# One row of the first group is loaded over the scalar queue, and the sync queue's loads have 32 and 32 rows

## The chip, the cores and the metric

The kernel runs on one core of one Trainium2 chip. A core has several engines that run their own instruction streams: VectorE (DVE in the profile), ScalarE (ACT), GpSimd (POOL), TensorE (PE, unused here) and SyncE (SP), which here only issues transfers. Transfers between the chip's main memory (HBM, "dram" in the names) and the on-chip memory of 128 partitions run on 16 DMA engines that all queues share. A transfer that SyncE issues goes on queue q1, one that ScalarE issues on queue q10.

The metric is device time in microseconds of one execution. The kernel before took 241.25 us, the median of three runs (240.55, 241.25, 241.26).

## What is computed

For each of 16 x 1024 = 16,384 tokens there are 8 router logits and a row of 512 numbers. The two largest logits give two weights that add up to one, and the row is written out twice, once times each weight, the smaller weight first:

```python
probs = np.exp(router_logits - logits_max)
probs = probs / np.sum(probs, axis=-1, keepdims=True)
topk_indices = np.argsort(probs, axis=-1)[..., -k:]          # k = 2
topk_probs = np.take_along_axis(probs, topk_indices, axis=-1)
topk_probs = topk_probs / np.sum(topk_probs, axis=-1, keepdims=True)
x_expanded = x[:, :, np.newaxis, :].repeat(k, axis=2)
return (x_expanded * topk_probs[..., np.newaxis]).astype(np.float32)
```

Everything is float32: 32 MiB of rows and 0.5 MiB of logits are read and 64 MiB are written.

## The kernel before

The 16,384 tokens are two groups (`GROUPS`, line 42): 65 x 128 tokens, then 63 x 128. In a group each of the 128 partitions has 65 (or 63) consecutive tokens, so "a row" below means one token on every partition: 512 numbers, 2 KB on each partition, 256 KB in all. The rows of a group lie in the tile `xs` (65 rows of space). A second tile, `osp`, has room for 18 rows of output, each twice as long as an input row.

`LOADS` (line 44) cuts a group's rows into transfers: 33 and 32 rows for the first group, 4, 28 and 31 for the second. Line 139 issues them. In the first group both go over the sync queue. Behind the first of them (line 142) the two parts of the logits are issued (lines 144 and 145), also on the sync queue, and `top2_weights` computes the weights `WA` from them: eleven small VectorE instructions, and then two sigmoids on ScalarE (lines 37 and 38). So the order on the sync queue is 33 rows, logits, logits, 32 rows.

`STORES` (line 47) cuts the output of a group into four stores: row from which it starts, number of rows, the tile that holds its output, and the place in that tile. Stores one and three of a group are built in `osp`; stores two and four are built in `xs` itself, over rows that are no longer needed. Line 164 multiplies rows by weights on VectorE, one instruction for each store, except that the third product of a group is cut in two (`FREE`, line 54): its first 2 rows go to a part of `osp` that the first store doesn't use, and the rest waits until the first store has landed. Of the first store's rows ScalarE does the last 5 (2 in the second group) as scaled copies (`ACT_ROWS`, line 156). Line 175 issues each store on the sync queue.

The second group's loads go to places in `xs` whose old contents must have been stored. Its first 4 rows go over the scalar queue (`late`, line 123): ScalarE does a copy that waits for the first group's third store to land (line 128) and then issues the load. The other two are on the sync queue, behind the first group's fourth store; the 28 rows wait for store two, the 31 rows for store four.

The instructions of each engine, and the transfers of each queue, stay in the order in which the program issues them. The fourth product of the first group (rows 49 to 64, `xs` from row 33 on) is the only one that reads row 64, the last of the group.

Of the kernel before, what the change touches and what calls it, by code (L numbers as in the profile page):

```python
# [1 line left out]

# [4 lines left out]

F32 = mybir.dt.float32
ALU = mybir.AluOpType
ACTF = mybir.ActivationFunctionType  # L10
P = 128


def top2_weights(nc, WA, dlt, room, logits, E):

    tt = nc.vector.tensor_tensor
    hi, lo, n = None, None, E  # L20
    while n > 1:
        n //= 2
        if hi is None:
            a, b = logits[:, :, 0:n], logits[:, :, n : 2 * n]
            nhi, nlo = room(n), b
            tt(nhi, a, b, op=ALU.max)  # L26
            tt(nlo, a, b, op=ALU.min)  # L27
        else:
            a, b = hi[:, :, 0:n], hi[:, :, n : 2 * n]
            nhi, nlo, tmp = room(n), room(n), room(n)  # L30
            tt(tmp, lo[:, :, 0:n], lo[:, :, n : 2 * n], op=ALU.max)  # L31
            tt(nlo, a, b, op=ALU.min)  # L32
            tt(nlo, nlo, tmp, op=ALU.max)  # L33
            tt(nhi, a, b, op=ALU.max)  # L34
        hi, lo = nhi, nlo
    tt(dlt, hi[:, :, 0], lo[:, :, 0], op=ALU.subtract)  # L36
    nc.scalar.activation(WA[:, :, 0], dlt, ACTF.Sigmoid, scale=-1.0)  # L37
    nc.scalar.activation(WA[:, :, 1], dlt, ACTF.Sigmoid, scale=1.0)  # L38

GROUPS = [65, 63]

LOADS = [[33, 32], [4, 28, 31]]
BASE = [0, 1]

STORES = [
    [(0, 16, "osp", 2), (16, 16, "xs", 0), (32, 17, "osp", 0), (49, 16, "xs", 33)],
    [(0, 16, "osp", 2), (16, 16, "xs", 0), (32, 15, "osp", 0), (47, 16, "xs", 32)],
]  # L50

L = 18

FREE = [2, 2]

ACT_ROWS = [5, 2]


@with_exitstack
def kernel(  # L60
    ctx: ExitStack,
    tc: tile.TileContext,
    x: bass.AP,
    router_logits: bass.AP,
    k: bass.AP,
    out: bass.AP,
):
    nc = tc.nc
    B, S, D = x.shape
    E = router_logits.shape[-1]  # L70
    N = B * S
    assert int(k) == 2 and E == 8 and N == P * sum(GROUPS)
    M = N // P

    x_v, o_v, rl_v = [], [], []
    t0 = 0
    for n in GROUPS:
        t1 = t0 + P * n
        x_v.append(
            x.rearrange("b s d -> (b s) d")[t0:t1].rearrange("(p m) d -> p m d", p=P)  # L80
        )
        o_v.append(
            out.rearrange("b s k d -> (b s) k d")[t0:t1].rearrange(
                "(p m) k d -> p m k d", p=P
            )
        )
        rl_v.append(
            router_logits.rearrange("b s e -> (b s) e")[t0:t1].rearrange(
                "(p m) e -> p m e", p=P
            )  # L90
        )
        t0 = t1

    wpool = ctx.enter_context(tc.tile_pool(name="wpool", bufs=1))
    xs = wpool.tile([P, max(GROUPS), D], F32)
    osp = wpool.tile([P, L, 2, D], F32)
    WA = wpool.tile([P, M, 2], F32)
    dlt = wpool.tile([P, M], F32)


    flat = osp.rearrange("p l k d -> p (l k d)")
    taken = [0]

    def room(n):
        o = taken[0]
        taken[0] += M * n
        return flat[:, o : o + M * n].rearrange("p (m n) -> p m n", n=n)

    logits = room(E)

    def place(where, at, n):

        if where == "osp":
            return osp[:, at : at + n]
        return xs[:, at : at + 2 * n, :].rearrange("p (r k) d -> p r k d", k=2)

    m0 = 0
    stores = []
    for g, G in enumerate(GROUPS):
        x0, r = BASE[g], 0  # L120
        for n in LOADS[g]:

            late = g == 1 and r == 0
            if late:


                rows = xs[:, x0 : x0 + 2, :]
                pause = nc.scalar.activation(rows, rows, ACTF.Copy)  # L128
                tc.add_manual_dep(
                    pause.ins,  # L130
                    stores[-2].ins.name,
                    mybir.DependencyInfo(
                        mybir.DependencyClass.Sync, mybir.DependencyReason.DATA
                    ),
                    reason="begin when the store ahead of the last has landed",
                )
                tc.keep_in_program_order(pause)
            queue = nc.scalar if late else nc.sync
            load = queue.dma_start(xs[:, x0 + r : x0 + r + n, :], x_v[g][:, r : r + n, :])  # L139
            tc.keep_in_program_order(load)  # L140
            r += n
            if g == 0 and r == LOADS[0][0]:
                n0 = GROUPS[0]
                tc.keep_in_program_order(nc.sync.dma_start(logits[:, :n0], rl_v[0]))  # L144
                tc.keep_in_program_order(nc.sync.dma_start(logits[:, n0:], rl_v[1]))
                top2_weights(nc, WA, dlt, room, logits, E)
        assert r == G
        for r, n, where, at in STORES[g]:
            og = place(where, at, n)

            again = where == "osp" and at == 0 and r > 0
            cuts = [0, FREE[g], n] if again else [0, n]
            if r == 0:
                cuts = [0, n - ACT_ROWS[g]]
                for j in range(n - ACT_ROWS[g], n):
                    for k2 in range(2):
                        nc.scalar.activation(  # L157
                            og[:, j, k2, :],
                            xs[:, x0 + r + j, :],
                            ACTF.Copy,  # L160
                            scale=WA[:, m0 + r + j, k2 : k2 + 1],
                        )
            for a, b in zip(cuts, cuts[1:]):
                nc.vector.tensor_tensor(  # L164
                    og[:, a:b],
                    xs[:, x0 + r + a : x0 + r + b, :]
                    .unsqueeze(2)
                    .to_broadcast([P, b - a, 2, D]),
                    WA[:, m0 + r + a : m0 + r + b, :]
                    .unsqueeze(3)  # L170
                    .to_broadcast([P, b - a, 2, D]),
                    op=ALU.mult,
                )

            stores.append(nc.sync.dma_start(o_v[g][:, r : r + n], og))  # L175
            tc.keep_in_program_order(stores[-1])
        m0 += G


# [1 line left out]
_INS = ['x', 'router_logits', 'k']  # L181
_OUTS = [((16, 1024, 2, 512), 'float32')]

_NUMBERS = {'k': 2}


# [26 lines left out]
```

## Time and profile before

| | |
|---|---|
| median of three runs | 241.25 us |
| the profiled execution | 240.59 us, of which the span from the first to the last instruction is 238.8 us |
| VectorE busy | 134.3 us (56% of the span) |
| ScalarE busy | 11.5 us |
| moved by DMA | 101.19 MB, 424 GB/s over the span |
| q1 (sync queue) | 2272 packets, 100.14 MB |
| q10 (scalar queue) | 144 packets, 1.05 MB |

In the timeline a row is: start, duration (both us), engine, line, operation, what it writes and reads. "SPq" and "ACTq" are the instructions that only issue a transfer; the duration there is that of issuing. In the chain of waits a row is start, duration, and what the end of the program waited for in that time. In the view of DMA issues a row gives the transfer, its size, and the time from issue to landing; the rows "q1" and "q10" give packets, megabytes and the time that these packets took as a share of 16 engines' time in that window. A packet is counted in the window in which it starts, so the share of a short window can be over 100%. In the view by windows the columns are the window, its length, the busy time of VectorE, ScalarE and GpSimd with the number of instructions, the clock, the DMA share and GB/s.

### The profile page before, as it was taken

To read this page: it belongs to the slowest core of one execution; us is meant where nothing else is said; L and a number is where in the kernel's file an instruction comes from. 1 tells how busy PE (TensorE), PEld (TensorE's weight loads), DVE (VectorE), ACT (ScalarE), POOL (GpSimd) and SP (SyncE) were. 2 spreads that over 40 slices of the span, in tenths; PEclk is the share of its full clock that TensorE was granted. 3 is DMA by queue.
4 is the path that set the end of the run, shared out by engine and by line. 5 is a ranking of instruction groups with operands and counts; after the bars stand their busy time and mean duration, and the time that the engine had idled before them with its cause. 6 is when DMAs were issued, how large, how long until landed. Compare 5 with 4: busy or idle time off the path is not lost.

```text
span 238.8 us, 118 instructions
## 1 busy us (share of the span) xinstructions
DVE 134.3 (56%) x21; ACT 11.5 (5%) x18; POOL 0.2 (0%) x4
## 2 busy tenths in 40 slices
DVE  0000799999599999200000019999966999950000
ACT  2000190000000000010000012000000000000000
POOL 0000000000000000000000000000000000000000
DMA  7999999898989899999999979798989897998984
GB/s 272 453 447 413 479 395 483 351 527 351 527 351 527 362 402 437 461 500 428 395 395 473 451 343 510 340 505 362 516 362 516 362 516 340 484 494 362 516 362 176
DMA packets 2416, 101.19 MB, mean 424 GB/s; under 512 B 240, under 2 KB 368, under 8 KB 496
## 3 DMA queue, kind: packets, MB, share of 16 engines
q1 hardware_dynamic: 2272, 100.14, 97.3%
q10 hardware_dynamic: 144, 1.05, 1.0%
HBM read 34.08 MB, written 67.11 MB: 424 GB/s over the span
## 4 chain that ended last, share of the span: by engine, by line
DMA 48%; DVE 40%; SPq 1%; issue 0%; ACT 0%; DVEq 0%
DVE osp L164 24%; DMA out_dram<-osp 19%; DMA xs<-in_x_dram 19%; DVE xs L164 14%; DMA osp<-in_router_logits_dram 10%; DVE osp L26 0%; DVE osp L27 0%; DVE osp L33 0%; DVE osp L31 0%; DVE osp L34 0%; DVE osp L32 0%; SPq L144 0%; SPq L139 0%; SPq L175 0%; ACT WA L38 0%
## 5 line engine op out<-in xcount | busy, mean ns | idle before, releaser
L164 DVE TENSOR_TENSOR osp<-xs,WA 128x2048 f32<-128x2048 f32 (+4 forms) x6 | 61.7, 10290 | 53.1 <-DMA xs<-in_x_dram 45.6
L164 DVE TENSOR_TENSOR xs<-xs,WA 128x16384 f32<-128x16384 f32 x4 | 68.9, 17226 | 0.3
L26 DVE TENSOR_TENSOR osp<-osp 128x512 f32<-128x512 f32 x1 | 0.7, 692 | 24.8 <-DMA osp<-in_router_logits_dram 24.8
L157 ACT ACTIVATE osp<-xs,WA 128x512 f32<-128x512 f32 x14 | 8.8, 707 | 38.0 <-DMA xs<-in_x_dram 38.0
L128 ACT ACTIVATE xs<-xs 128x1024 f32<-128x1024 f32 x1 | 1.1, 1057 | 68.0 <-DMA out_dram<-osp 68.0
L37 ACT ACTIVATE WA<-dlt 128x128 f32<-128x128 f32 x1 | 0.3, 316 | 26.7 <-DVE dlt L36 26.7
L37 ACT ACT_TABLE_LOAD x1 | 1.3, 1283 | 0.7 <-PEq L194 0.7
L27 DVE TENSOR_TENSOR osp<-osp 128x512 f32<-128x512 f32 x1 | 0.7, 691 | 0.0
L31 DVE TENSOR_TENSOR osp<-osp 128x256 f32<-128x256 f32 (+1 forms) x2 | 0.7, 350 | 0.0
L34 DVE TENSOR_TENSOR osp<-osp 128x256 f32<-128x256 f32 (+1 forms) x2 | 0.7, 350 | 0.0
L32 DVE TENSOR_TENSOR osp<-osp 128x256 f32<-128x256 f32 (+1 forms) x2 | 0.7, 350 | 0.0
L33 DVE TENSOR_TENSOR osp<-osp 128x256 f32<-128x256 f32 (+1 forms) x2 | 0.7, 350 | 0.0
L36 DVE TENSOR_TENSOR dlt<-osp 128x128 f32<-128x128 f32 x1 | 0.3, 291 | 0.0
L38 ACT ACTIVATE WA<-dlt 128x128 f32<-128x128 f32 x1 | 0.3, 298 | 0.0
L194 POOL MEMSET const-bfloat16-1.0<- 128x1 bf16 x1 | 0.1, 101 | 0.0
L194 POOL MEMSET const-uint8-127<- 128x1 uint8 x1 | 0.1, 101 | 0.0
L194 POOL MEMSET const-float32-0.0<- 128x1 f32 x1 | 0.1, 98 | 0.2 <-issue 0.2
L194 POOL MEMSET const-float32-1.0<- 128x1 f32 x1 | 0.1, 98 | 0.0
## 6 DMA issues: line engine op xcount, KB each, us to landing
out_dram<-osp SPq DMA_DIRECT2D x1, 8704.0 KB, 23.6
xs<-in_x_dram SPq DMA_DIRECT2D x1, 8448.0 KB, 22.6
xs<-in_x_dram SPq DMA_DIRECT2D x1, 7936.0 KB, 37.0
out_dram<-osp SPq DMA_DIRECT2D x1, 7680.0 KB, 23.3
xs<-in_x_dram SPq DMA_DIRECT2D x1, 7168.0 KB, 45.0
xs<-in_x_dram ACTq DMA_DIRECT2D x1, 1024.0 KB, 25.2
osp<-in_router_logits_dram SPq DMA_DIRECT2D x1, 260.0 KB, 22.9
osp<-in_router_logits_dram SPq DMA_DIRECT2D x1, 252.0 KB, 23.0
```

What stands on the lines that cost most here:

```text
L26: tt(nhi, a, b, op=ALU.max)
L27: tt(nlo, a, b, op=ALU.min)
L31: tt(tmp, lo[:, :, 0:n], lo[:, :, n : 2 * n], op=ALU.max)
L32: tt(nlo, a, b, op=ALU.min)
L33: tt(nlo, nlo, tmp, op=ALU.max)
L34: tt(nhi, a, b, op=ALU.max)
L36: tt(dlt, hi[:, :, 0], lo[:, :, 0], op=ALU.subtract)
L37: nc.scalar.activation(WA[:, :, 0], dlt, ACTF.Sigmoid, scale=-1.0)
L128: pause = nc.scalar.activation(rows, rows, ACTF.Copy)
L157: nc.scalar.activation(og[:, j, k2, :], xs[:, x0 + r + j, :], ACTF.Copy, scale=WA[:, m0 + r + j, k2 : k2 + 1],)
L164: nc.vector.tensor_tensor(og[:, a:b], xs[:, x0 + r + a : x0 + r + b, :] .unsqueeze(2) .to_broadcast([P, b - a, 2, D]), WA[:, m0 + r + a : ...
L194: nc = _bacc.Bacc("TRN2", target_bir_lowering=False, num_devices=1)
```

## The change

The first group's rows are loaded in three transfers, of 32, 32 and 1 rows, where there were two of 33 and 32. The two of 32 rows keep their places on the sync queue, the logits stand between them as before. The one row, row 64, is issued by ScalarE, and gets a dependency on the first load, so that it isn't issued before that has landed. In ScalarE's program it stands behind the two sigmoids and ahead of the ten scaled copies of the first store. The fourth product of the first group waits for it as for the other loads.

```diff
-LOADS = [[33, 32], [4, 28, 31]]
+LOADS = [[32, 32, 1], [4, 28, 31]]
...
-            queue = nc.scalar if late else nc.sync
+            alone = g == 0 and r == G - 1
+            queue = nc.scalar if late or alone else nc.sync
             load = queue.dma_start(xs[:, x0 + r : x0 + r + n, :], x_v[g][:, r : r + n, :])
+            if alone:
+                tc.add_manual_dep(
+                    load.ins,
+                    first.ins.name,
+                    mybir.DependencyInfo(
+                        mybir.DependencyClass.Sync, mybir.DependencyReason.DATA
+                    ),
+                    reason="begin when the first load has landed",
+                )
+            if g == r == 0:
+                first = load
             tc.keep_in_program_order(load)
```

## The prediction

> **What bounds the kernel now.** I read the page's head and its queue part first, since they say which resource is full.
>
> ```profile
> span 238.8 us, 118 instructions
> DVE 134.3 (56%) x21; ACT 11.5 (5%) x18; POOL 0.2 (0%) x4
> DMA packets 2416, 101.19 MB, mean 424 GB/s; under 512 B 240, under 2 KB 368, under 8 KB 496
> q1 hardware_dynamic: 2272, 100.14, 97.3%
> q10 hardware_dynamic: 144, 1.05, 1.0%
> ```
>
> q1 holds everything that SyncE issues, q10 the one load that ScalarE issues. Together their packets fill 98.3% of 16 engines' span, while VectorE works 56% of it. So the kernel is a stream of bytes, and a change of order pays only where the stream has a hole. To look for holes I took issue times from the timeline, landings from the chain of waits and the view of DMA issues, and the length of one packet from narrow windows of that view.
>
> ```profile
> 2.18 0.65 SPq L139 DMA_DIRECT2D xs<-in_x_dram  x1
> 79.66 0.38 SPq L175 DMA_DIRECT2D out_dram<-osp  x1
> 212.55 0.33 SPq L175 DMA_DIRECT2D out_dram<-xs  x1
> ...
> 1.71 23.01 DMA osp<-in_router_logits_dram
> 41.28 22.18 DMA out_dram<-osp
> 97.31 45.02 DMA xs<-in_x_dram
> 157.69 23.52 DMA out_dram<-osp
> ...
> xs<-in_x_dram SPq DMA_DIRECT2D x1, 41.9
> out_dram<-xs SPq DMA_DIRECT2D x1, 25.4
> q1 hardware_dynamic: 16, 1.05, 241.8%
> q1 hardware_dynamic: 16, 0.92, 105.8%
> q10 hardware_dynamic: 16, 0.13, 15.4%
> q1 hardware_dynamic: 11, 0.38, 110.7%
> q1 hardware_dynamic: 240, 8.11, 94.3%
> ```
>
> The last five rows are windows 1, 2, 2, 0.8 and 19.9 us long. The share is of 16 engines over the window, and a packet counts where it starts, so share x window x 16 / packets is the length of one packet: 2.418 us for 64 KB (16 rows stored, 32 loaded), 2.116 for 56 KB (28 rows), 0.308 for the 8 KB packets of q10, 1.288 for the 34 KB halves of the 17-row store, 1.251 for the 33 KB halves of the first load. Between 33,792 and 65,536 B the slope is 1.167 us / 31,744 B = 0.0368 ns a byte and the intercept 0.009 us: a packet costs its bytes and almost nothing else. A transfer of 128 partitions gives each engine 8 packets (16 for the two made of halves).
>
> Now landing to landing, against these packets:
> - logits (1.71 + 23.01 = 24.72) to first store (63.45): 38.73 us for load two and store one, 16 x 2.418 = 38.69. Surplus 0.04.
> - on to store three, which releases ScalarE's copy at 103.34 (row below): 39.89 for 8 x 2.418 + 16 x 1.288 = 39.95. Surplus -0.06.
> - on to the 28-row load (142.33): 38.99 for 8 x 2.418 + 8 x 2.116 + 8 x 0.308 = 38.74. Surplus 0.25, in the stretch where the scalar queue's load runs.
> - on to group 1's first store (181.21): 38.88 for the 31-row load, 8 x 2.342 by the slope, and 19.34: 38.08. Surplus 0.80.
> - on to the last store (212.55 + 25.4 = 237.95): 56.74 for 56.83 (8 packets of 60 KB at 2.267, again by the slope). Surplus -0.09.
>
> What is left for any reordering is thus the start, 1.05 us of surplus in the second half, and the end.
>
> ```profile
> 1.75:2.40 0.65, 0.00 (x0) 0.25 (x1) 0.00 (x0) 1.00 3.09 832
> 234.00:235.20 1.20, 0.00 (x0) 0.00 (x0) 0.00 (x0) 1.00 0.13 55
> ```
>
> The first window (its sixth value is the DMA share) holds the 16 first packets: 3.09 x 0.65 = 2.01 us each against 1.251 later, a ramp of 0.76 us. The second holds 0.13 x 1.2 x 16 = 2.5 us, one packet: fifteen engines started their last packet before 234.0, one over a microsecond later. That one engine sets the end.
>
> **The change part by part.** *The sync loads.* Load one loses 256 KB and its halves: 8 x 2.418 instead of 16 x 1.251 us per engine, 19.34 for 20.02, so -0.67. The logits and load two behind it come 0.67 us earlier. *The new load.* 128 packets of 2 KB, 8 per engine, at 0.009 + 2048 x 0.0368 ns = 0.084 us each: +0.67. The bytes are the same, and the packet counts too (16 -> 8 + 8 per engine), so the sum over the stream is 0.0. One more completion packet per engine is at most the 0.009 intercept.
>
> *When it is issued.* The dependency names load one, but on ScalarE the load stands behind both sigmoids and ahead of the ten scaled copies:
>
> ```profile
> 24.82 0.69 DVE L26 TENSOR_TENSOR osp<-osp 128x512 f32<-128x512 f32 x1 [24.82 <-DMA osp<-in_router_logits_dram]
> 28.96 0.30 ACT L38 ACTIVATE WA<-dlt 128x128 f32<-128x128 f32 x1
> 29.16 6.22 ACT L157 ACTIVATE osp<-xs,WA 128x512 f32<-128x512 f32 x10
> 103.34 1.06 ACT L128 ACTIVATE xs<-xs 128x1024 f32<-128x1024 f32 x1 [67.96 <-DMA out_dram<-osp]
> 104.43 0.37 ACTq L139 DMA_DIRECT2D xs<-in_x_dram  x1
> xs<-in_x_dram ACTq DMA_DIRECT2D x1, 1024.0 KB, 25.2
> 29.29 11.89 DVE L164 TENSOR_TENSOR osp<-xs,WA 128x11264 f32<-128x11264 f32 x1 [0.58 <-ACT WA L38]
> 79.67 17.23 DVE L164 TENSOR_TENSOR xs<-xs,WA 128x16384 f32<-128x16384 f32 x1
> ```
>
> The sigmoids end at 29.26, or 28.6 with the 0.67; load one has landed some 6 us before, so its wait is already over and holds nothing. The issue takes 0.37 us and delays the ten copies by that. They end at 35.4 now, VectorE's first product, which the same store waits for, at 41.18: 5.8 us of cover. Without it the store would be 0.37 us later.
>
> *Landing of the row.* The existing scalar load takes 25.2 us for 8 packets per engine: each takes its turn after one 64 KB packet of q1, 8 x (2.418 + 0.308) = 21.8 plus the way there. With 0.084 for 0.308 it is 23.4 us, so the row lands near 52. Its only user is the product at 79.67: 27 us of cover.
>
> *First product and store one.* The first product starts and the first store is issued 0.67 earlier, 40.6 for 41.28. Store one needs engines that are busy with load two until that lands (2.18 + 41.9 = 44.1; about 43.8 in the new order, with some five of the eight row packets ahead). The stretch above has a surplus of 0.04, so there is no hole for the earlier store to fill: gain 0. By the time store one has landed, all eight row packets are through as well, so it lands at 63.45 as before. VectorE's third product and store three hang on that landing; store three is issued at 79.66, 3 us ahead of store two's landing, and everything later keeps its place.
>
> *What the trace doesn't show* is 2 KB packets between 64 KB ones, or a load that starts with 64 KB packets. For the first, the nearest row is the q10 load: 8 packets per engine, with a surplus of 0.25 us in its stretch; the other end is -0.06. For the second, the ramp may stay (one wait per engine: 0), halve with the number of pieces (-0.38), or grow with the packet's bytes (+0.71). I take 0 for both, because 8 KB packets run at the stream's price to 0.03 us each and the ramp is paid once per engine, and keep both ends.
>
> The sum: -0.67 + 0.67 + 0.01 = 0.0 us on the profiled execution, whose 240.59 us are a span of 238.8 and 1.8 around it. The runs shown have 241.25 as median, 0.66 above it, and lie in two places, 240.55 and 241.25; a changed kernel without effect gives a median between them. I take 241.1.
>
> **The rivals.** *Slower: the second queue disturbs the stream.* The surplus is nil up to the scalar load of group 1 (0.04, -0.06) and 0.25 + 0.80 in the stretches in which it runs and that follows. If such a load puts the engines out of step and the lag shows at the next hand-over from a load to a store, a second one, right at the hand-over from load two to store one, costs up to the same 1.05: 241.25 + 1.05 = 242.3. It becomes slower as counted here once it passes 0.72. For it speaks that nothing else separates these stretches in the queue; against it that the 0.80 comes 13 us and more after that load has landed (104.43 + 25.2 = 129.6), and the last stretch has none.
>
> *Slower: a DMA's fixed price is paid.* Every DMA takes time before its first packet; where nothing else runs, it shows:
>
> ```profile
> 0.72 0.42 SPq L139 DMA_DIRECT2D xs<-in_x_dram  x1
> 1.00:1.75 0.75, 0.00 (x0) 0.75 (x1) 0.00 (x0) 1.00 0.00 0
> ```
>
> From the first issue at 0.72 to 1.75 no engine moves a packet: 1.0 us. Were the engines held for that by the one DMA more, the time would be 241.25 + 1.0 = 242.3. Against it: the stretch with the surplus of 0.25 starts two DMAs, and the one from the logits on, with 0.04, two as well, so other packets cover that price. The Trainium skill (DMA: Bandwidth & Descriptors, "Anatomy of one DMA") puts about 2.0 us of fixed cost on each DMA, fitted on the GpSimd path; laid bare it would make an estimated 243.2 here, which those stretches do not bear out.
>
> *Faster: the start and the first store.* If half the ramp goes with half the pieces (-0.38), and if the executions at 241.25 have a hole of up to 0.67 before store one that this profile lacks, the earlier product fills it: 241.25 - 1.05 = 240.2. For it speaks only the spread of the runs; against it a stretch that closes within 0.04.
>
> *The change doesn't do what it says.* The row is issued 6 us after load one has landed, behind the sigmoids. As the cover is 27 us, that changes no time.
>
> **How the numbers follow.** No measurable change 0.51; disturbed stream 0.26 (242.3); fixed price 0.03 (242.3); faster start 0.20 (240.2). Within 0.3% (0.72 us, about what a measurement of this kernel can tell from no change) is the first case; the sum of the next two is slower. The likeliest case alone spans 240.5 to 241.7. The range of 8 in 10 takes in both neighbours, 240.0 to 242.4.
>
> **What would show it.** Right: q10 with 288 packets; the logits landing near 24.05, the first product near 28.6, store one issued near 40.6 yet landing near 63.4; the row landing near 52; the stretches of the second half with surpluses no larger than now. Wrong: store one landing by more than 0.3 us off 63.45 (the ramp, or the row's packets, have a price), VectorE's product at 79.67 waiting for the row, or the one engine at the end further behind than 1.2 us. A time outside 240.5 to 241.7 with all landings of group 0 in place would mean that the lag of single engines, not the stream, decides.

## The result, and the profile after

The changed kernel is slower: 241.84 us, the median of nine runs (241.39 to 242.38), against 240.34 us for the kernel before in nine runs beside it (239.98 to 241.26). The ratio is 1.0057, with a 95% interval of 1.0041 to 1.0073; here and below it is estimated from all runs and need not be the quotient of the two medians. The profiled execution took 241.94 us.

The page's head and queue part of the changed kernel:

```profile
span 240.2 us, 120 instructions
DMA packets 2432, 101.19 MB, mean 421 GB/s; under 512 B 256, under 2 KB 384, under 8 KB 640
q1 hardware_dynamic: 2144, 99.88, 96.6%
q10 hardware_dynamic: 288, 1.31, 1.3%
```

The same bytes are moved, in the packets that were expected; the span is 1.4 us longer. The rows of the timeline, the chain of waits and the view of DMA issues that answer to those of before:

```profile
28.13 0.37 ACTq L140 DMA_DIRECT2D xs<-in_x_dram  x1
2.10 0.69 SPq L140 DMA_DIRECT2D xs<-in_x_dram  x1
...
1.64 22.46 DMA osp<-in_router_logits_dram
40.65 23.15 DMA out_dram<-osp
97.66 46.91 DMA xs<-in_x_dram
159.93 22.73 DMA out_dram<-osp
...
xs<-in_x_dram SPq DMA_DIRECT2D x1, 42.1
xs<-in_x_dram ACTq DMA_DIRECT2D x1, 256.0 KB, 16.4
out_dram<-xs SPq DMA_DIRECT2D x1, 25.4
```

The logits land 0.62 us earlier (24.10 for 24.72), store one is issued 0.63 earlier (40.65 for 41.28). Yet load two lands at 44.2, not earlier than before (44.1), and store one lands at 63.80, 0.35 later than before. Further on the distance grows: the 28-row load lands at 144.57 for 142.33 (+2.24), the second group's first store at 182.66 for 181.21 (+1.45), the last store at 213.99 + 25.4 = 239.4 for 237.95 (+1.4).

Where the first 0.35 us comes from shows in the length of the last packet that each engine has of load two. The view of DMA issues in the window in which these sixteen packets start, of the kernel before (0.70 us long) and then of the changed one (0.75 us):

```profile
q1 hardware_dynamic: 16, 1.05, 345.9%
```

```profile
q1 hardware_dynamic: 16, 1.05, 351.1%
q10 hardware_dynamic: 13, 0.03, 9.1%
```

Share x window x 16 / packets gives 2.421 us before, the length of every 64 KB packet, and 2.633 us after: 0.21 us more in the mean of the engines, while the row's packets on q10 have 0.084 us each as worked out. So an engine loses 0.2 us in the mean on its last piece of load two.

Most of the 2.24 us at the 28-row load comes much later. When store three lands and releases ScalarE's copy, the distance is still 0.45 us (103.79 for 103.34). Store four then lands 27.8 us after its issue before (at 124.7), and 29.7 us after it in the changed kernel (at 127.0), 2.2 us later. In this stretch the scalar queue's four rows run beside store four, and two engines fall behind: their 64 KB packets take 2.57 us (0.402 x 0.8 x 16 / 2) instead of 2.42. The first row is of the kernel before, the others are of the changed one; the last is a window of 0.80 us from 118.9 us on, with one packet of each of the two:

```profile
out_dram<-xs SPq DMA_DIRECT2D x1, 27.8
...
103.79 1.06 ACT L128 ACTIVATE xs<-xs 128x1024 f32<-128x1024 f32 x1 [69.00 <-DMA out_dram<-osp]
out_dram<-xs SPq DMA_DIRECT2D x1, 29.7
q1 hardware_dynamic: 2, 0.13, 40.2%
```

What makes them fall behind, no run isolates: no kernel with long last packets of load two goes without the scalar queue's load.

A further loss shows near 160 us, where the second group's first store takes over from its last load. The view by windows, before and then after:

```profile
159.90:160.70 0.80, 0.80 (x1) 0.00 (x0) 0.00 (x0) 1.00 2.85 1229
160.70:161.60 0.90, 0.90 (x1) 0.00 (x0) 0.00 (x0) 1.00 0.17 73
```

```profile
159.90:160.70 0.80, 0.76 (x1) 0.00 (x0) 0.00 (x0) 1.00 0.19 79
160.70:161.60 0.90, 0.90 (x1) 0.00 (x0) 0.00 (x0) 1.00 2.39 1019
```

The sixth value is the DMA share by start of packets. Before, 2.85 x 0.8 x 16 = 36 us of packets start in the first window: fifteen engines go straight from load to store. After, one 62 KB packet starts there, and fourteen start in the second window, 0.8 us later. Those engines have nothing to do, since the store is issued only at 159.93 (157.69 before): its product waits for the 28-row load, and that counts as landed when the slowest of the sixteen engines is through.

The end, by windows, after the change:

```profile
234.10:235.00 0.90, 0.00 (x0) 0.00 (x0) 0.00 (x0) 1.00 2.52 1092
235.00:236.00 1.00, 0.00 (x0) 0.00 (x0) 0.00 (x0) 1.00 0.15 66
236.00:237.00 1.00, 0.00 (x0) 0.00 (x0) 0.00 (x0) 1.00 0.15 66
```

Fifteen packets start in the first window (2.52 x 0.9 x 16 / 2.418), one of them the next-to-last of the slowest engine; one engine starts its last packet between 235 and 236, one between 236 and 237. Before, fifteen had started it before 234.0. So most engines are about 1 us later, and the last one 1.4 us.

### The profile page after: what moved, and what is told of

It is laid out like the page before. It is cut to its first block, busy times and chain, and to the rows that moved or that the text cites. A ratio compares the mean times of both kernels' runs of the same rounds, so it can differ in the third digit from the quotient of the medians.

```text
span 240.2 us, 120 instructions
## 1 busy us (share of the span) xinstructions
DVE 134.3 (56%) x21; ACT 11.6 (5%) x18; POOL 0.2 (0%) x4
## 4 chain that ended last, share of the span: by engine, by line
DMA 48%; DVE 40%; SPq 0%; issue 0%; ACT 0%; DVEq 0%; ACTq 0%
DVE osp L176 24%; DMA xs<-in_x_dram 20%; DMA out_dram<-osp 19%; DVE xs L176 14%; DMA osp<-in_router_logits_dram 9%; DVE osp L26 0%; DVE osp L27 0%; DVE osp L33 0%; DVE osp L34 0%; DVE osp L32 0%; DVE osp L31 0%; SPq L156 0%; SPq L140 0%; SPq L187 0%; ACT WA L37 0%
## 6 DMA issues: line engine op xcount, KB each, us to landing
xs<-in_x_dram ACTq DMA_DIRECT2D x1, 256.0 KB, 16.4
```

## The experiments

All kernels were timed beside the kernel before on the same chip, whose median lay between 240.40 and 240.64 us there. The column "lead" of the table at the end is the reading that the later experiments were made for.

### Four kernels on the second queue

Theory A was that the row on the second queue disturbs the stream, theory B that a first load in 64 KB packets does. *The row on the sync queue:*

```diff
-            queue = nc.scalar if late or alone else nc.sync
+            queue = nc.scalar if late else nc.sync
```

with the added dependency taken out.

> The one row goes over the sync queue right behind load two, with no dependency; the two loads of 32 rows stay. Theory A (the row on the second queue disturbs the hand-over from load two to store one, which leaves the engines apart): no disturbance, so the time of before, ratio 0.998 to 1.002, store one landing at 63.4 us. Theory B (the start with 64 KB packets costs the time): still slow as the change is, ratio about 1.006.

Measured: 241.81 us, ratio 1.0034 (1.0011 to 1.0058). Still slow without a second queue in the first group, and the last packets of load two are as long as in the changed kernel; the window is 0.60 us:

```profile
q1 hardware_dynamic: 16, 1.05, 439.7%
```

4.397 x 0.6 = 2.638 us in the mean. Theory A in this form falls, by the packets rather than by the time, since the lower end of the interval, 1.0011, is inside what theory A expected.

*33 and 31 rows, the row on the scalar queue:*

```diff
-LOADS = [[32, 32, 1], [4, 28, 31]]
+LOADS = [[33, 31, 1], [4, 28, 31]]
```

> The first load has 33 rows again, the second 31, and the last row stays on the scalar queue behind the first load's landing. Theory A (the row on the second queue): still slow, ratio about 1.006, store one landing at 63.8 us. Theory B (the start with 64 KB packets): the time of before, ratio 1.000.

Measured: 240.96 us, ratio 1.0009 (0.9984 to 1.0034). Not told from before, though the row's packets run between those of load two as in the change. That speaks for theory B; theory A's 1.006 is outside the interval.

*The row behind load two's landing:*

```diff
-            if g == r == 0:
+            if g == 0 and r == LOADS[0][0]:
                 first = load
```

> As the change, but the row waits for load two to land, so that its packets run between those of store one alone. Theory A in its narrow form (only the hand-over from one transfer to the next on the sync queue is disturbed): nothing lost, ratio 0.999 to 1.002. In its wide form (any mixing of two queues puts the engines apart): ratio 1.004 or more. Theory B: ratio about 1.006.

Measured: 241.20 us, ratio 1.0008 (0.9986 to 1.0031), and no long packets. Window of 0.60 us:

```profile
q1 hardware_dynamic: 16, 1.05, 403.9%
```

2.423 us in the mean. This start is the one of the changed kernel, 64 KB packets and all, so theory B in its plain form (1.006) falls too. What came out as expected is theory A in its narrow form: the time is not lost when the row is away from the hand-over from load two to store one.

*The kernel before with all loads on the sync queue:*

```diff
-            queue = nc.scalar if late else nc.sync
+            queue = nc.sync
```

> The kernel before with the second group's four rows on the sync queue too, so that no second queue is ever in use. Theory A in its wide form: the surplus of 0.25 and 0.80 us in the second half is from that load as well and goes, ratio about 0.996 (1.05 of 240.3 us). If the second queue costs nothing in itself: ratio 1.000. Theory B says nothing of it: 1.000.

Measured: 240.49 us, ratio 0.9992 (0.9968 to 1.0016). The ratio of 0.996 that theory A in its wide form promised is outside the interval, and the profiled execution has the span of before, 238.8 us. The second queue is not what the surplus of the second half comes from.

### Four kernels on the first load's size

*The change once more.* No edit.

> The changed kernel once more, on the same chip as the three runs below and with its own profile. Both theories: slower than before, ratio 1.004 to 1.007; the profile again with the 28-row load landing over 1 us late and store one of the second group issued when the engines are already idle, if that bubble belongs to the change and not to one execution.

Measured: 241.29 us, ratio 1.0019 (0.9994 to 1.0044): on this chip the loss is about 0.7 us in the medians and its interval reaches no change. The profiled execution (241.11 us) has long last packets too, but fewer (2.49 us in the mean), store three lands as late as in the first profile (ScalarE's copy starts at 103.76), but the 28-row load lands at 143.05, 0.7 us late and not 2.2, and the second group's first store is issued at 158.41, in time. So the idle engines near 160 us belong to some executions only; what both profiles share is load two's long packets and engines that lag after them.

*32 rows first, then 33, and no row alone:*

```diff
-LOADS = [[33, 32], [4, 28, 31]]
+LOADS = [[32, 33], [4, 28, 31]]
```

> The kernel before with its two first loads exchanged, 32 rows first and then 33, and no row alone. Theory A (the row's small packets at the hand-over from load two to store one cost the time, over whichever queue they go): ratio 0.998 to 1.002. Theory B (a first load of 32 rows in 64 KB packets, with everything behind it 0.67 us earlier, costs it): ratio about 1.005.

Measured: 241.64 us, ratio 1.0019 (0.9988 to 1.0050). The median is 1.1 us above that of before, but the twelve runs lie from 239.58 to 242.36 and the interval decides nothing. The trace says more: store one was issued at 40.51, and load two's last packets, 33 KB here, took 1.40 us in the mean instead of 1.251. The window is 0.80 us:

```profile
q1 hardware_dynamic: 16, 0.54, 175.2%
```

So long last packets need no row alone.

*33 and 31 rows, and the row behind them on the sync queue:*

```diff
-LOADS = [[32, 32, 1], [4, 28, 31]]
+LOADS = [[33, 31, 1], [4, 28, 31]]
...
-            queue = nc.scalar if late or alone else nc.sync
+            queue = nc.scalar if late else nc.sync
```

> 33 and 31 rows on the sync queue, and the last row on the sync queue right behind them. Theory A (the row's small packets at that hand-over): slow as with 32 and 32 rows, ratio 1.003 to 1.006. Theory B (the first load of 32 rows): the time of before, ratio 0.999 to 1.002.

Measured: 240.53 us, ratio 1.0007 (0.9986 to 1.0028). No loss that can be told. Together with the row on the scalar queue behind 33 and 31 rows, this clears the row where the first load has 33 rows: neither its queue nor its 2 KB packets behind load two cost time there.

*The change with the 28 rows cut into 16 and 12,* so that the second group's first product begins earlier:

```diff
-LOADS = [[32, 32, 1], [4, 28, 31]]
+LOADS = [[32, 32, 1], [4, 16, 12, 31]]
```

> The change, with the second group's 28-row load cut into 16 and 12, so that the first product of that group has its rows some 7 us earlier and its store can't come late. Theory C (the lag reaches the end through that late store, which leaves most engines idle for 0.6 us): ratio about 1.002, no idle engines near 160 us. If the lag of single engines alone sets the end: ratio 1.005 as the change.

Measured: 242.60 us, ratio 1.0059 (1.0030 to 1.0087), against the expectation of 1.002. No engine idles near 160 us any more, and yet the kernel is the slowest so far. The store was issued at 150.90 and queued for 9 us. The sixteen last packets of the load ahead of it, 62 KB, in a window of 1.30 us:

```profile
q1 hardware_dynamic: 16, 1.02, 226.5%
```

2.265 x 1.3 = 2.94 us in the mean where 62 KB take 2.342: an engine lost 0.60 us in the mean. In the kernel before, where this store is issued at 157.69, only one lost time. Windows of 0.80 us with all sixteen and of 0.10 us with that one:

```profile
q1 hardware_dynamic: 16, 1.02, 299.1%
...
q1 hardware_dynamic: 1, 0.06, 196.8%
```

The mean is 2.393, the one 1.968 x 0.1 x 16 = 3.15 us, 0.81 more than the others. This agrees with the surplus of 0.80 us that the prediction had found and not explained.

That gave theory D: a store that is queued well ahead of the end of a load makes the last packets of that load long. Under it the change is slow because its earlier logits bring store one 0.63 us earlier, while load two ends no earlier by as much.

### Four kernels on the time of the stores

ScalarE's share of a first store is varied, and nothing else. A row less on ScalarE is a row more on VectorE, 1.08 us of work, and the store comes about that much later, with the next store behind it.

*The change, store one later:*

```diff
-ACT_ROWS = [5, 2]
+ACT_ROWS = [4, 2]
```

> The change with ScalarE doing 4 rows of the first store instead of 5: VectorE's first product has a row more, 1.08 us, and store one is issued near 41.75 us instead of 40.65, still ahead of the end of load two. Theory D (a store that is issued over some 2 us before an engine is through with its load slows that engine's last packets, so the earlier store is what costs): the long last packets of load two near 40 us are gone and the ratio is 1.000, a store issued later makes the kernel faster. Theory B in its plain form (64 KB packets in the first load cost it): ratio 1.003 to 1.005 as before this edit.

Measured: 239.66 us, ratio 0.9979 (0.9958 to 1.0001), 0.7 us below the kernel before (the interval just reaches no change) and 2.2 below the time of the change, by a *later* store. Store one is issued at 41.65, and load two's last packets, in a window of 0.80 us:

```profile
q1 hardware_dynamic: 16, 1.05, 302.2%
q10 hardware_dynamic: 16, 0.03, 10.5%
```

2.418 us, with the row's packets between them as before. Ten of the twelve runs lie between 239.50 and 239.92, two near 241.4.

*The kernel before, store one earlier* (`ACT_ROWS = [6, 2]`, loads untouched):

> The kernel before, loads untouched, with ScalarE doing 6 rows of the first store instead of 5: store one is issued near 40.2 us instead of 41.28. Theory D: the last packets of load two get long (mean 0.1 to 0.3 us per engine) and the ratio is 1.003 or more, without any change of the loads. Theory B: ratio 1.000.

Measured: 242.05 us, ratio 1.0063 (1.0041 to 1.0085): the loss of the change, without any change of the loads. Store one is issued at 40.21. The 28-row load and the second group's first store in the chain of waits, and load two's last packets in a window of 0.60 us:

```profile
97.83 46.58 DMA xs<-in_x_dram
159.77 22.73 DMA out_dram<-osp
...
q1 hardware_dynamic: 16, 1.05, 491.4%
```

4.914 x 0.6 = 2.948 us: 0.53 us lost by an engine in the mean. The 28-row load lands at 144.41 and the second group's first store is issued at 159.77, as in the changed kernel. So moving store one forward is enough to bring about the late landing of a load 80 us on.

*The kernel before, the second group's first store later* (`ACT_ROWS = [5, 1]`):

> The kernel before with ScalarE doing 1 row of the second group's first store instead of 2: that store is issued near 158.8 us instead of 157.7, 1.2 us before the first engine is through with its load. Theory D: the slowest engine's long last packet near 158 us (0.81 us) goes, ratio 0.996 to 0.998, so this beats the kernel before. If the lag has nothing to do with the store's issue: ratio 1.000; if 1.2 us are too little for the store to start: 1.002.

Measured: 239.69 us, ratio 0.9975 (0.9955 to 0.9996), as expected. The profiled execution took 240.73 us, 1 us above the median: there the store was issued at 159.62, and fifteen engines started its packets only after 160.45, having run dry. So the gain is shown by the times; how the executions of 239.5 to 239.8 us get it, no profile shows.

*The change with both later* (`ACT_ROWS = [4, 1]`):

> The change with both first stores issued 1.08 us later (4 rows and 1 row on ScalarE). Theory D: ratio 0.996 to 0.999, faster than the changed kernel by about 1.5 us. Theory B: 1.002 or more.

Measured: 239.44 us, ratio 0.9951 (0.9934 to 0.9969), more than the 0.996 to 0.999 expected. It beats both kernels, and its seven runs lie within 239.34 and 239.52. Chain and the end by windows:

```profile
97.23 44.88 DMA xs<-in_x_dram
158.54 21.63 DMA out_dram<-osp
...
233.00:234.10 1.10, 0.00 (x0) 0.00 (x0) 0.00 (x0) 1.00 2.20 953
234.10:235.00 0.90, 0.00 (x0) 0.00 (x0) 0.00 (x0) 1.00 0.00 0
235.00:236.00 1.00, 0.00 (x0) 0.00 (x0) 0.00 (x0) 1.00 0.00 0
```

All sixteen engines start their last packet in the first window (2.20 x 1.1 x 16 / 2.418 = 16.0). No engine lags, and the 28-row load lands at 142.11.

### Three kernels on what was still open

*The change with all products as they are, store one held back* by six copies on ScalarE, in place on spent scratch:

```diff
+            idle = None
+            if g == 0 and r == 0:
+                for _ in range(IDLE):
+                    idle = nc.scalar.activation(osp[:, 0], osp[:, 0], ACTF.Copy)
+                    tc.keep_in_program_order(idle)
             stores.append(nc.sync.dma_start(o_v[g][:, r : r + n], og))
+            if idle is not None:
+                tc.add_manual_dep(
...
```

> The change with all its products as they are, but store one also waits for six copies of 1024 numbers that ScalarE does in place on spent scratch, behind its ten scaled copies; that puts its issue near 41.5 us instead of 40.65 and moves nothing else. Theory D (the issue time of the store against the end of the loads): as with the product a row longer, no long last packets near 40 us, ratio 0.996 to 1.000. If the longer product had helped in another way (VectorE's or ScalarE's work beside the loads): ratio 1.003 to 1.006 as the change.

Measured: 240.81 us, ratio 1.0002 (0.9986 to 1.0018). The issue came out at 41.17, nearer to the change's than meant, and the time is that of the kernel before, which issues at 41.28. The packets are back to 2.434 us in the mean. So the issue time alone takes the long packets away; the longer product is not needed for it. The interval lies below that of the change's first measurement (from 1.0041), though not below that of its second (from 0.9994).

*The kernel before with both stores later* (`ACT_ROWS = [4, 1]`):

> The kernel before, loads untouched, with both first stores a row later (4 rows and 1 row on ScalarE): store one issued near 42.35 us, 0.65 us before the first engine is through with load two. Theory D: if that is still in time, 239.4 us as the change with the same edit, ratio 0.995, and the loads of the change are worth nothing in themselves; if a store needs some 1 us from issue to first packet, engines idle by up to 0.4 us near 43 us and the ratio is 0.996 to 0.999, so the change is worth what its earlier logits leave room for.

Measured: 242.54 us, ratio 1.0064 (1.0040 to 1.0087). Both expectations miss: it is 3 us slower than the change with the same edit. Store one was issued at 42.26 and landed at 63.38, so the first hand-over lost nothing; the 28-row load landed at 143.31, 1.2 us later than in that kernel, and the second group's store, a row longer, was issued at 159.73. Part of the 1.2 us shows in store four. The sixteen packets that start between 107.4 and 108.0 us, one to an engine, are long, and so are its sixteen last ones, in a window of 0.60 us as well:

```profile
q1 hardware_dynamic: 16, 1.05, 451.1%
...
q1 hardware_dynamic: 16, 1.05, 495.3%
```

These are 2.71 us for 2.418, and 2.97 us, where the last packets of store four take 2.84 in the change with the same edit. Why, no run shows. The profiled execution took 240.75 us, and four of the twelve runs lie below 241; what costs the other eight their 241.9 to 242.8 us, no profile here shows.

*The cut load again, with its early store held back* by nineteen such copies (`LOADS` as in the kernel with 16 and 12 rows):

> The change with the second group's loads as 4, 16, 12 and 31 rows, where the first store of that group was issued at 150.9 us and all sixteen engines had long last load packets (0.60 us in the mean) near 158 us. Now that store also waits for nineteen copies on ScalarE, to about 158.7 us; the products stay. Theory D: those sixteen long packets are gone, ratio 1.001 to 1.004 instead of 1.006. If the cut load itself made them long: they stay, ratio 1.006.

Measured: 241.71 us, ratio 1.0036 (1.0019 to 1.0054), within what was expected. Not one of the sixteen packets was long; fifteen of them are in this window of 0.80 us, at 2.342 us each:

```profile
q1 hardware_dynamic: 15, 0.95, 274.5%
```

So the queued store had made them long and not the cut. But the store came out later than meant, at 160.18, and most engines idled before it.

### The runs by lead

The lead is the landing of load two less the issue of store one, in the profiled execution. The landing is later by the added time itself, so the next column does without it: it goes from the issue to where the latest of load two's sixteen last packets would end at its normal length. The fourth column is the mean length of these packets above the normal one (2.418 us for 64 KB, 2.342 for 62 KB, 1.251 for 33 KB).

| kernel | lead, us | without added time, us | added, us | ratio to before |
|---|---|---|---|---|
| before, both stores later | 1.7 | 1.3 | 0.00 | 1.0064 |
| change, store one later | 2.2 | 1.6 | 0.00 | 0.9979 |
| change, both stores later | 2.2 | 1.6 | 0.00 | 0.9951 |
| 33, 31, row on sync | 2.2 | 1.7 | 0.00 | 1.0007 |
| 33, 31, row on scalar | 2.6 | 2.0 | 0.01 | 1.0009 |
| change, store one held back | 2.7 | 2.2 | 0.02 | 1.0002 |
| before | 2.8 | 2.3 | 0.00 | 1 |
| before, all on sync | 2.8 | 2.3 | 0.00 | 0.9992 |
| before, group two's store later | 2.8 | 2.3 | 0.01 | 0.9975 |
| change, row behind load two | 2.8 | 2.4 | 0.01 | 1.0008 |
| change, row on sync | 3.4 | 2.4 | 0.22 | 1.0034 |
| change, second time | 3.4 | 2.7 | 0.07 | 1.0019 |
| the change | 3.6 | 2.6 | 0.21 | 1.0057 |
| change, 28 rows cut | 3.6 | 2.6 | 0.08 | 1.0059 |
| change, 28 rows cut, store held back | 3.6 | 2.7 | 0.18 | 1.0036 |
| 32, 33 | 3.9 | 3.0 | 0.15 | 1.0019 |
| before, store one earlier | 4.4 | 3.4 | 0.53 | 1.0063 |

Up to 2.8 us of lead next to nothing is added, from 3.4 us on something always is. Without the added time the split is at 2.4 and 2.6 us, with one exception. The row on the sync queue has the same 2.4 us as the row behind load two, differs from it only in when and over which queue the row goes, and has 0.22 us added for 0.01. So a row between load two and an early store one has a share in the loss, though long packets come without it too (the last two kernels of the table).

In the five profiles with 0.15 us or more added, the last of the second group's 28 rows land at 144.2 to 144.7 us; in the other twelve at 142.1 to 143.4. The ratio follows only in part, and the first row shows that a short lead alone doesn't make a fast kernel. The later hand-over has its say: in the profile of 33, 31 and the row on scalar (241.95 us, 1 us above its median) one engine's last packet ahead of the second group's first store took 3.97 us instead of 2.342. The window is 0.30 us:

```profile
q1 hardware_dynamic: 1, 0.06, 82.6%
```

## Why the prediction was wrong

*The time.* The forecast was 241.1 us, no measurable change. The measured 241.84 us lies inside the range of 240.0 to 242.4 us, but that is luck: both were reckoned from 241.25 us, the median of three runs, and nine runs of the kernel before have 240.34. From there the forecast would be 240.2 us and the range end at 241.5. How large the loss is stays open: 1.5 us in the first measurement, 0.7 us in the second, whose interval reaches no change.

*The bound.* Right: the stream of bytes is full, and q10 has 288 packets.

*Sum over the stream.* Right as far as it goes: the row's packets and the sync loads cancel, and the row with its DMA costs nothing that can be told where the hand-over is left alone (1.0008, row behind load two).

*When the row is issued and landed.* It was issued at 28.13, not 28.6, and without delay for the copies: the issue ran beside the first sigmoid and did not wait for the two to end.

```profile
28.12 0.32 ACT L37 ACTIVATE WA<-dlt 128x128 f32<-128x128 f32 x1 [26.11 <-DVE dlt L36]
28.34 0.30 ACT L38 ACTIVATE WA<-dlt 128x128 f32<-128x128 f32 x1
28.55 6.24 ACT L169 ACTIVATE osp<-xs,WA 128x512 f32<-128x512 f32 x10
```

It landed after 16.4 us, at 44.5, not near 52: it was through as soon as load two was. The turns with one 64 KB packet each did not go on into store one: 49 of the row's 128 packets start between 43.0 and 44.0 us. Neither made its product wait; that cover was ample as argued.

*First product and store one.* This step failed: "there is no hole for the earlier store to fill: gain 0". The shift was right (40.65 for 40.6). But load two landed at 44.2 and not at 43.8, and store one at 63.80 and not at 63.45. The gain of 0 was taken for the whole effect: an earlier store has a price of its own, a term that the sum did not have. It is 0.21 us on an engine's last packet, in the mean, in the changed kernel, and 0.53 us where the store alone was moved 1.07 us forward.

*"Everything later keeps its place".* This failed with it. The 0.35 us at store one's landing became 2.24 at the 28-row load, most of it during store four, where two engines fell behind; by what step is open. Then most engines idled for up to 0.8 us, because a load lands with its slowest engine and the next store waits for the product of that load. The surplus of 0.80 us between the 31-row load and the store behind it was in the table of stretches, and was left as a lag of unknown cause; the packet of 3.15 us shows it as the same kind of price, paid by one engine in the kernel before.

*The rivals.* The slower rival had the place (the hand-over from load two to store one) and nearly the time (242.3 for 241.84, by luck of the base: from 240.34 it would be 241.4), with the wrong cause: the second queue. Three runs clear it at that hand-over: still slow with the row on the sync queue (1.0034), no faster with no second queue at all (0.9992), and as slow as the change with the loads untouched (1.0063). A fixed price of about 1 us for one DMA more is outside the interval of the kernel that carries that DMA away from the hand-over (1.0031 at most, 0.75 us). The fixed cost of 2.0 us on each DMA that the Trainium skill (DMA: Bandwidth & Descriptors, "Anatomy of one DMA") gives, fitted on the GpSimd path, lies outside that interval as well. The faster rival's better half, the earlier store, has the opposite sign. Not cleared is the scalar queue's load of four rows as what lets a lag grow during store four.

*The marks.* Store one landing more than 0.3 us off 63.45, and the engine at the end further behind, were named as what would show it wrong. The first came out at 0.35 us. The second came too: before, one engine landed 1.2 us behind the other fifteen, and after the change the last one 1.8 us behind fourteen.

## What to carry to other kernels

On a full stream, issuing a store earlier is not free: here a store issued 3.4 us or more before the load ahead of it landed lengthened that load's last packets, and the best kernel issued store one 2.2 us before. Look at the slowest DMA engine and not at the mean, since every landing and the end wait for it; a lag of 0.2 us from one hand-over came out as 1.5 us here. Where a lag in the profile has no explanation, test what stands queued behind it before calling it chance.

## What the runs showed of the hardware that was not expected

A store that is queued on the same engines can slow the end of a load: 0.60 us in the mean of sixteen engines with 9 us of queueing, 0.81 us on one engine only when the store was issued 0.7 us ahead of that engine's last packet. It doesn't always: in the changed kernel's profile one engine, too, starts the last packet of the 31-row load 0.7 us after the issue of the store behind it, and that packet has its normal 2.34 us. There the store was issued so late that the other engines were through with the load. Why a queued store does this, no view shows, and why at a middle lead some engines pay and others don't is open as well.

The other direction costs too: in all seventeen profiles the last packets of group one's fourth store take 2.50 to 2.97 us in the mean, also in the kernel with all loads on the sync queue (2.67). These packets, with the second group's loads behind them, in windows of 0.70 us (kernel before) and 0.60 us (change with both stores later):

```profile
q1 hardware_dynamic: 16, 1.05, 378.4%
```

```profile
q1 hardware_dynamic: 16, 1.05, 473.5%
```

2.65 and 2.84 us for packets of 2.418. No run tried to take this away.
